# Squares of the sub-norm read from PSUM behind the value product, and the embedding's tiles placed two by two among other projections

## The chip, the cores and the metric

The kernel runs on one core of a Trainium2 chip. The metric is the time of one execution on the device, in microseconds (us). A figure below in which a trace is read belongs to one profiled execution.

## The reference, cut to what matters

```python
def reference(x, p, ...):
    h = x                                           # 512 x 1024, fp32
    for i in range(2):
        hn = rmsnorm(h, norm_mix_g[i])
        h = h + (even_mixer if i == 0 else odd_mixer)(hn, ...)
        hn = rmsnorm(h, norm_mlp_g[i])
        h = h + jnp.square(relu(hn @ w_mlp_up[i])) @ w_mlp_down[i]
        gate = sigmoid(rmsnorm(h, norm_ple_g[i]) @ w_ple_gate[i])
        h = h + (p[i] @ w_ple_proj[i]) * gate       # p[i]: 512 x 256, the embedding
    return rmsnorm(h, final_norm_g)
# even_mixer: 8 stick-breaking heads, and 4 differential heads with
#   attn = softmax1 - lam * softmax2;  o = attn @ v (128 wide)
#   o = rmsnorm(o, subln_g) * (1 - lambda_init)     # the sub-norm
# and a projection w_out of all heads' outputs
```

Layer 0 has the even mixer, layer 1 the odd one (dilated windows). The product `p[i] @ w_ple_proj[i]` depends on nothing else and may be computed at any time.

## The kernel before, in words

All matrix products keep fp32 precision by a split: an operand is rounded to a high part (`hi`, `wh`, `ph`) and what is left is a low part (`lo`, `wl`, `pl`), and `mm3` issues three matmuls, lines L138 (high times high), L141 (low of the one operand) and L142 (low of the other).

**Weights.** `wload` fetches a block of weights into a tile `raw` (two buffers); `wsplit` makes its high part on ScalarE (ACT, L122), and its low part on GpSimd (POOL, L126) in two halves, the first for k=0 and the second for k=1 of a block with two steps of contraction. The tiles `wh` and `wl` have three buffers each, and all blocks take them in turn, the two parts `ph`, `pl` of the embedding `p` among them:

```python
hi = (pool or wpool).tile([P, nk, n], F32R, tag="wh", name=nm("wh"), bufs=bufs)   # bufs = 3
lo = (pool or wpool).tile([P, nk, n], F32R, tag="wl", name=nm("wl"), bufs=bufs)
nc.scalar.activation(hi, src, AF.Copy)
for x in range(2):
    kx = slice(x * nk // 2, (x + 1) * nk // 2)
    nc.gpsimd.tensor_tensor(lo[:, kx], src[:, kx], hi[:, kx].bitcast(F32), op=ALU.subtract)
```

**Stages of the mixer.** Layer 0 has four groups of heads, in the order 2, 3, 0, 1: groups 2 and 3 are differential, 0 and 1 stick-breaking. `attend(g)` gives the attention of a group as a list of small steps, and `interleave(units, total, steps)` issues them evenly among the units of another generator, each of which is some matmuls: the projection `project` of the next group (value columns, then two blocks each of q and k). The program of a stage is then one fixed order for TensorE (PE); ACT, VectorE (DVE) and POOL follow orders that a scheduler set ahead of the run. In the last stage of layer 0, attention of group 1, the units are those of `out_first`, the first part of the output projection, four blocks of 128x768 in two halves with two output tiles each.

**The embedding's projection.** `ple_units(layer)` computes `p @ w_ple_proj` as two blocks c of four tiles of 128x512; a tile is six matmuls (k=0, 1), an evacuation from PSUM on ACT (L365) and a store to DRAM (`pjd`). All of layer 0's stand ahead of `project(1)` in the stage of attend(0); all of layer 1's stand ahead of `out_first` in the stage of attend(1). They yield once behind each three matmuls.

**The sub-norm.** Of a differential group, `combine(x)` (x = 0, 1) issues the value product into a PSUM bank `pv` and copies it to `o` (L605). Two steps later `subnorm(x)` squares `o` (L618), rounds the squares to a high part (L619), leaves the low part to DVE (L620), and sums over the partitions by two matmuls with a matrix of ones (L622, L623).

Of the kernel before, what the change touches and what calls it, by code (L numbers as in the profile page):

```python
# [3 lines left out]

# [1 line left out]

# [6 lines left out]
F32 = mybir.dt.float32  # L13
# [49 lines left out]
def trunk(  # L63
# [284 lines left out]
    def ple_units(layer):  # L348
        raw = wpool.tile([P, 2 * KT * P], F32, tag="raw", name=nm("raw"), bufs=2)
        nc.sync.dma_start(raw[:, 0:2 * S].rearrange("p (k c) -> p k c", k=2), pT[layer].rearrange("k p c -> p k c"))  # L350
        ph, pl = wsplit(raw, 0, 2, S)
        raw = wload(w_proj[layer])
        for c in range(2):
            wh, wl = wsplit(raw, c, 2, 512)
            for i in range(4):
                acc = ps("mm")
                sl = slice(i * P, (i + 1) * P)
                for k in range(2):
                    if layer < DEPTH - 1:
                        mm3(acc, wh[:, k, sl], wl[:, k, sl], ph[:, k], pl[:, k], k == 0, k == 1)  # L360
                    else:
                        mm3(acc, ph[:, k, sl], pl[:, k, sl], wh[:, k], wl[:, k], k == 0, k == 1)
                    yield 2.0
                t = mix[0].tile([P, S], F32, tag="bias", name=nm("pjt"), bufs=4) if i % 2 else t2k("tmp2")
                nc.scalar.activation(t, acc, AF.Copy)  # L365
                nc.sync.dma_start(pjd[layer, 4 * c + i], t)

    KLB = 2
    kl_i = [0]
# [2 lines left out]
    def mixer(layer, norm, nxt):  # L372
# [32 lines left out]
        lead_in = ["sc", "sc", "mm", "mm", "pv", "tp"]  # L405
        oT = [mpool.tile([P, S], F32, tag=f"o{k}", name=nm("o"), bufs=1) for k in range(KT)]

        def project(g, cur):
            kind = "dil" if layer else ("sb" if g < 2 else "diff")
            start = not first  # L410
            first.append(g)
            v = mpool.tile([P, QT, 512], F32R, tag="v", name=nm("v"), bufs=2)

            def values():
                raw = wload(next_block())
                banks = [ps(lead_in.pop(0)) if start else ps("mm") for _ in range(QT // 2)]
                accs = [b[:, c:c + 256] for b in banks for c in (0, 256)]
                for half in range(2):
                    wh, wl = wsplit(raw, half, 4, 256)
                    if half and "rcol" not in stat:  # L420
                        stat["rcol"] = tok_cols(stat["rstd"])
                    for t in range(QT):
                        for k in range(4):
                            ah, al = ahl[4 * half + k]
                            tk = slice(t * P, (t + 1) * P)
                            mm3(accs[t], ah[:, tk], al[:, tk], wh[:, k], wl[:, k],
                                half == 0 and k == 0 and t % 2 == 0, half == 1 and k == 3 and t % 2 == 1)
                            yield 1.0
                        if half == 1 and t % 2 == 1:
                            evacuate_values(t - 1, accs[t - 1])  # L430
                            evacuate_values(t, accs[t])

            def evacuate_values(t, acc):
                sc = stat["rcol"][:, t:t + 1]
                if kind == "diff":
                    src = acc
                    vh, vl = v[:, t, 0:256], v[:, t, 256:512]
                else:
                    src = acc.rearrange("p (a c) -> p a c", a=4)
                    vv = v[:, t, :].rearrange("p (a b c) -> p a b c", a=4, b=2)  # L440
                    vh, vl = vv[:, :, 0, :], vv[:, :, 1, :]
                nc.scalar.activation(vh, src, AF.Copy, scale=sc)
                nc.vector.scalar_tensor_tensor(vl, src, sc, vh.bitcast(F32), op0=ALU.mult, op1=ALU.subtract)  # L443

            heads = []

            def queries_keys():
                qscale = -0.5 * HD ** -0.5 if kind == "sb" else 0.5 * HD ** -0.5
                qk, waiting = [], []
                for isq in (True, False):  # L450
                    src = next_block()
                    lo_eng[0] = nc.vector if start else nc.gpsimd
                    blk = blk0 if isq and start and not layer else block(src, KT, P)
                    lo_eng[0] = nc.gpsimd
                    accs = [ps(lead_in.pop(0)) if start else ps("mm") for _ in range(2)]
                    if start and isq:
                        yield from lin_units(accs, blk, ahl, 0, KT, True)
                        waiting = accs
                        continue
                    if start and not layer:  # L460
                        prepare()
                    for i, acc in enumerate(accs):
                        yield from lin_units([acc], [blk[i]], ahl, 0, KT, False)
                        if waiting:
                            statistics()
                            for x, held in enumerate(waiting):
                                evacuate(True, x, held, qk, qscale)
                            waiting = []
                        evacuate(isq, i, acc, qk, qscale)

            def evacuate(isq, i, acc, qk, qscale):
                rstd = stat["rstd"]
                f = t2k("tmp")
                nc.vector.scalar_tensor_tensor(f, acc, qscale if isq else -0.5, rstd, op0=ALU.mult, op1=ALU.mult)
                lower, upper = slice(0, 64), slice(64, 128)
                if isq:
                    qq = []
                    for a, b in ((lower, upper), (upper, lower)):
                        q = mpool.tile([P, S], F32R, tag="qq", name=nm("qq"), bufs=5)
                        nc.scalar.activation(q[a], f[a], AF.Copy)  # L480
                        nc.vector.tensor_tensor(q[b], f[a], q[a].bitcast(F32), op=ALU.subtract)
                        qq.append(q)
                    qk.append(qq)
                else:
                    for s, (a, b) in enumerate(((lower, upper), (upper, lower))):
                        kl = klz[s][kl_i[0] % KLB]
                        kh = mpool.tile([P, S], F32R, tag="kh", name=nm("kh"), bufs=5)
                        nc.scalar.activation(kh[a], f[a], AF.Copy)
                        nc.scalar.activation(kh[b], f[a], AF.Copy)
                        nc.vector.tensor_tensor(kl[a], f[a], kh[a].bitcast(F32), op=ALU.subtract)  # L490
                        heads.append((qk[i][s], kh, kl))
                    kl_i[0] += 1
            cur.extend((g, kind, v, heads))
            if start:
                yield from queries_keys()
                yield from values()
            else:
                yield from values()
                yield from queries_keys()
# [55 lines left out]
        def attend(g, kind, v, heads):  # L555
# [1 line left out]
            nh = 2 if kind == "diff" else 4  # L557
            pts = [(pt_i[0] + x) % 2 for x in range(nh)]
            pt_i[0] += nh
            bias, ready = {}, {}  # L560

            def weights(x, i, evict):
                n = P * (i + 1)
# [34 lines left out]
            def combine(x):  # L598
                hi, lo = pth[pts[x]], ptl[pts[x]]
                if kind == "diff":  # L600
                    vh = lambda j: v[:, j, P * x:P * x + P]
                    vl = lambda j: v[:, j, 256 + P * x:256 + P * x + P]
                    op = pv([(vh, hi), (vh, lo), (vl, hi)])
                    o = oT[2 * g + x]
                    nc.scalar.activation(o, op, AF.Copy)  # L605
                    return
                vs = lambda j: v[:, j, P * x:P * x + P]
                op = pv([(vs, hi), (vs, lo)])
# [5 lines left out]

            def subnorm(x):
                o = oT[2 * g + x]
                hi, rs, lo = t2k("tmp2", dtype=F32R), t2k("tmp2"), t2k("tmp2", dtype=F32R)
                nc.scalar.activation(rs, o, AF.Square)  # L618
                nc.scalar.activation(hi, rs, AF.Copy)  # L619
                nc.vector.tensor_tensor(lo, rs, hi.bitcast(F32), op=ALU.subtract)  # L620
                mp = ps("pv")
                nc.tensor.matmul(mp, ones_r, hi, start=True, stop=False)  # L622
                nc.tensor.matmul(mp, ones_r, lo, start=False, stop=True)  # L623
# [29 lines left out]
                    ohl.append(split_tile(oT[tiles[len(ohl)]]))  # L653
                yield cost

        def out_first():
            for c in range(4):
                blk = block(w_outa[layer, c], 6, P)
                accs = [ps("mm") for _ in range(2)]
                for k, i in [(k, i) for k in range(6) for i in range(2)] if c == 0 else \  # L660
# [4 lines left out]
                    yield 2.0  # L665
                    if k == 5:
                        nc.vector.tensor_tensor(h[2 * c + i], h[2 * c + i], accs[i], op=ALU.add)

        cur = []
        run(project(groups[0], cur))  # L670
        for n, g in enumerate(groups[1:]):
            steps = attend(*cur)
            cur = []
            if layer == 0 and n == 2:
                interleave(chain(ple_units(0), project(g, cur)), 132.0, steps)
            else:
                interleave(project(g, cur), 100.0, steps)
        if layer == 0:
            interleave(chain(spread(ple_units(1), 2), out_first()), 100.0, attend(*cur))
        else:  # L680
            interleave(out_first(), 72.0, attend(*cur))
        ohl += [split_tile(oT[k]) for k in tiles[6:8]]
# [347 lines left out]
```

## Time and profile before

| what | value |
|---|---|
| time of the kernel, median of 3 runs | 1309.97 us (1309.74 to 1310.89) |
| time of the profiled execution | 1308.87 us |
| its span in the trace | 1307.1 us |
| granted clock, mean | 0.998 |
| stages that the change touches, in the trace | about 70 to 262 us |

The span runs from the first to the last instruction of the trace; the profiled execution took 1.8 us more, which lies around it. Busy time is the union of an engine's instructions. Matmuls are pipelined: a row's duration (0.39 us for 512 columns) is longer than the distance from one start to the next (0.23 us) where nothing is waited for, so time that PE loses is read from the distances of starts.

### The profile page before, as it was taken

The page shows a single profiled execution, that of the slowest core. Times are in us where ns is not written, and L with a number is a line of the kernel's source. Part 1 is how long each engine was busy: PE and PEld are TensorE (multiplying, and loading weights), DVE is VectorE, ACT ScalarE, POOL GpSimd, SP SyncE. Part 2 cuts the span into 40 slices and gives each one's busy share as a digit, 9 for nine tenths or more (in the row PEclk, how much of TensorE's full clock was granted, in tenths as well). Part 3 has the DMA queues.
Part 4 walks back from the last instruction along what each step waited for, and adds up shares of the span by engine and source line. Part 5 has one row for each costly group of instructions (what it writes and reads, how often), then busy time and mean ns, then how long its engine had stood idle before and what let it go on. Part 6 is the DMA issues. An engine that isn't in the chain of part 4 may idle for free.

```text
span 1307.1 us, 18561 instructions
## 1 busy us (share of the span) xinstructions
PE 1283.7 (98%) x7256; PEld 1117.4 (85%) x7256; DVE 973.5 (74%) x1623; ACT 686.0 (52%) x1117; POOL 189.8 (15%) x160
## 2 busy tenths in 40 slices
PE   9999999999999999999999999999999999999997
PEld 7988787888998989988889888788899898998876
DVE  7788888778848869845767877887784885994566
ACT  6666768554535334333456666765553443533344
POOL 2433434410000000000024333222000000000001
PEclk9999999999999999999999999999999999999999
DMA  6421423223232322323432222212223123232241
GB/s 217 135 81 50 140 93 115 89 82 112 86 108 97 102 92 97 129 97 101 157 112 96 84 89 78 69 57 95 99 97 124 70 97 129 73 122 97 97 145 65
DMA packets 28040, 133.20 MB, mean 102 GB/s; under 512 B 3312, under 2 KB 4048, under 8 KB 15280
## 3 DMA queue, kind: packets, MB, share of 16 engines
q1 hardware_dynamic: 27952, 132.01, 29.5%
q8 instruction: 57, 0.93, 0.3%
q14 instruction: 31, 0.25, 0.1%
HBM read 125.63 MB, written 6.37 MB: 101 GB/s over the span
## 4 chain that ended last, share of the span: by engine, by line
PE 85%; DVE 8%; ACT 4%; issue 1%; DMA 1%; SPq 0%; POOL 0%; ACTq 0%; DVEq 0%; POOLq 0%
PE mm L138 10%; PE mm L141 10%; PE mm L142 10%; PE sc L141 6%; PE sc L142 6%; PE sc L138 6%; PE pv L142 5%; PE pv L141 5%; PE pv L138 5%; PE tp L141 5%; PE tp L142 5%; PE tp L138 5%; PE pv L551 2%; PE tp L532 2%; PE sc L506 1%
## 5 line engine op out<-in xcount | busy, mean ns | idle before, releaser
L122 ACT ACTIVATE wh<-raw 128x1024 fp32r<-128x1024 f32 (+1 forms) x168 | 173.4, 1036 | 226.9 <-PE mm L141 63.0
L126 POOL TENSOR_TENSOR wl<-raw,wh 128x512 fp32r<-128x512 f32 (+1 forms) x132 | 177.1, 1364 | 309.3 <-ACT wh L122 303.6
L138 PE MATMUL mm<-hi,wh 128*128 128x512 f32 x472 | 187.0, 396 | 0.6 <-DVE v L443 0.4
L142 PE MATMUL mm<-hi,wl 128*128 128x512 f32 x472 | 184.8, 392 | 0.1
L141 PE MATMUL mm<-lo,wh 128*128 128x512 f32 x472 | 184.6, 391 | 0.0
L128 DVE TENSOR_TENSOR wl<-raw,wh 128x1024 fp32r<-128x1024 f32 x102 | 124.5, 1224 | 41.3 <-ACT wh L122 34.8
L142 PEld LDWEIGHTS mm<-hi,wl 128*128 128x128 f32 x472 | 88.6, 188 | 20.1 <-POOL wl L126 0.5
L138 PEld LDWEIGHTS mm<-hi,wh 128*128 128x128 f32 x472 | 88.7, 188 | 17.3 <-DVE v L443 0.6
L141 PEld LDWEIGHTS mm<-lo,wh 128*128 128x128 f32 x472 | 88.7, 188 | 15.6
L526 ACT ACTIVATE e<-e,mn 128x128 f32<-128x128 f32 (+3 forms) x96 | 53.8, 561 | 65.4 <-DVE mn L523 65.0
L754 ACT ACTIVATE wh<-raw 128x1024 fp32r<-128x1024 f32 x48 | 50.7, 1057 | 69.6 <-PE tp L141 35.1
L733 DVE TENSOR_TENSOR ul<-u,uh 128x1792 fp32r<-128x1792 f32 (+1 forms) x32 | 58.4, 1824 | 23.4 <-ACT uh L732 23.4
L732 ACT ACTIVATE uh<-u 128x1792 fp32r<-128x1792 f32 (+1 forms) x32 | 49.4, 1544 | 48.9 <-DVE u L728 48.7
L138 PE MATMUL sc<-hi,wh 128*128 128x512 f32 x184 | 71.9, 391 | 0.9 <-ACT hi L182 0.9
L141 PE MATMUL sc<-lo,wh 128*128 128x512 f32 x184 | 72.1, 392 | 0.3 <-DVE lo L183 0.3
L142 PE MATMUL sc<-hi,wl 128*128 128x512 f32 x184 | 71.8, 390 | 0.0
L721 ACT ACTIVATE u<-u 128x512 f32<-128x512 f32 x64 | 39.4, 625 | 53.8 <-DVE u L720 53.8
L142 PE MATMUL pv<-uh,wl 128*128 128x256 f32 (+1 forms) x224 | 67.4, 301 | 0.0
L142 PE MATMUL sc<-uh,wl 128*128 128x256 f32 (+1 forms) x224 | 67.3, 301 | 0.0
L141 PE MATMUL pv<-ul,wh 128*128 128x256 f32 (+1 forms) x224 | 67.2, 300 | 0.0
L141 PE MATMUL sc<-ul,wh 128*128 128x256 f32 (+1 forms) x224 | 67.2, 300 | 0.0
L138 PE MATMUL pv<-uh,wh 128*128 128x256 f32 (+1 forms) x224 | 66.6, 297 | 0.0
(259 smaller groups left out, 3645.4 us busy)
## 6 DMA issues: line engine op xcount, KB each, us to landing
raw<-in_w_up_dram SPq DMA_DIRECT2D x32, 1024.0 KB, 4.9
raw<-in_w_down_dram SPq DMA_DIRECT2D x32, 1024.0 KB, 4.9
raw<-in_w_in_dram SPq DMA_DIRECT2D x23, 1024.0 KB, 4.9
raw<-in_w_gate_dram SPq DMA_DIRECT2D x8, 1024.0 KB, 5.0
bias<-urow SPq DMA_DIRECT2D x24, 256.0 KB, 3.9
raw<-in_w_outa_dram SPq DMA_DIRECT2D x8, 768.0 KB, 4.2
pj<-pjd SPq DMA_DIRECT2D x16, 256.0 KB, 5.0
h<-in_xT_dram SPq DMA_DIRECT2D x8, 256.0 KB, 5.6
```

What stands on the lines that cost most here:

```text
L122: nc.scalar.activation(hi, src, AF.Copy)
L126: nc.gpsimd.tensor_tensor(lo[:, kx], src[:, kx], hi[:, kx].bitcast(F32), op=ALU.subtract)
L128: nc.vector.tensor_tensor(lo, src, hi.bitcast(F32), op=ALU.subtract)
L138: mm = nc.tensor.matmul(acc, lh, rh, start=start, stop=False)
L141: nc.tensor.matmul(acc, lh, rl, start=False, stop=False)
L142: nc.tensor.matmul(acc, ll, rh, start=False, stop=stop)
L526: nc.scalar.activation(e[:, 0:n], e[:, 0:n], AF.Exp, scale=-1.0, bias=mn, accum_out=s)
L532: nc.tensor.transpose(tp[:, j * P:(j + 1) * P], e[:, j * P:(j + 1) * P], ident)
L721: nc.scalar.activation(ui, ui, AF.Square, scale=0.5)
L732: nc.scalar.activation(uh[:, parts], u[:, parts], AF.Copy)
L733: nc.vector.tensor_tensor(ul[:, parts], u[:, parts], uh[:, parts].bitcast(F32), op=ALU.subtract)
L754: nc.scalar.activation(hi, src, AF.Copy)
```

## The change

The squares: `combine` now squares the PSUM bank twice, into `rs` (fp32) and into the rounded `hi`, copies `o` behind them, and forms `lo` on DVE; `subnorm` only takes these tiles up.

The embedding's tiles: of layer 0 two tiles are issued behind each of the four evacuations of q and k in `project(1)`; of layer 1 four tiles stand ahead of `out_first`, and one behind each of the first four additions to `h` in it. A tile's second yield stands behind its evacuation, and all tiles evacuate into the tag "bias" with four buffers, where every second one went to "tmp2".

```diff
@@ ple_units
-                    yield 2.0
-                t = mix[0].tile([P, S], F32, tag="bias", name=nm("pjt"), bufs=4) if i % 2 else t2k("tmp2")
+                    if k == 0:
+                        yield 2.0
+                t = mix[0].tile([P, S], F32, tag="bias", name=nm("pjt"), bufs=4)
                 nc.scalar.activation(t, acc, AF.Copy)
                 nc.sync.dma_start(pjd[layer, 4 * c + i], t)
+                yield 2.0
@@ project
-        def project(g, cur):
+        def project(g, cur, extra=iter(())):
...
                         evacuate(isq, i, acc, qk, qscale)
+                        yield from islice(extra, 4)
@@ combine (differential)
                     o = oT[2 * g + x]
+                    hi, rs, lo = t2k("tmp2", dtype=F32R), t2k("tmp2"), t2k("tmp2", dtype=F32R)
+                    nc.scalar.activation(rs, op, AF.Square)
+                    nc.scalar.activation(hi, op, AF.Square)
                     nc.scalar.activation(o, op, AF.Copy)
+                    nc.vector.tensor_tensor(lo, rs, hi.bitcast(F32), op=ALU.subtract)
+                    squares[x] = (rs, hi, lo)
                     return
@@ subnorm
-                hi, rs, lo = t2k("tmp2", dtype=F32R), t2k("tmp2"), t2k("tmp2", dtype=F32R)
-                nc.scalar.activation(rs, o, AF.Square)
-                nc.scalar.activation(hi, rs, AF.Copy)
-                nc.vector.tensor_tensor(lo, rs, hi.bitcast(F32), op=ALU.subtract)
+                rs, hi, lo = squares.pop(x)
@@ out_first
-        def out_first():
+        def out_first(extra=iter(())):
...
                         nc.vector.tensor_tensor(h[2 * c + i], h[2 * c + i], accs[i], op=ALU.add)
+                        yield from islice(extra, 2)
@@ mixer
-                interleave(chain(ple_units(0), project(g, cur)), 132.0, steps)
+                interleave(project(g, cur, ple_units(0)), 132.0, steps)
...
-            interleave(chain(spread(ple_units(1), 2), out_first()), 100.0, attend(*cur))
+            extra = ple_units(1)
+            interleave(chain(spread(islice(extra, 8), 2), out_first(extra)), 100.0, attend(*cur))
```

Three places show how this moves the instructions. A name's last number counts the tiles; `x2` stands for two such instructions in a row; lines are those of the kernel that a row is of.

The first is ACT's order around the second sub-norm (x=1) of group 3; `kh` is evacuated keys, `pv_1571` the bank with the value product. Before:

```order
L489 ACTIVATE kh_1560<-tmp_1558 64x512
L488 ACTIVATE kh_1564<-tmp_1558 64x512
L489 ACTIVATE kh_1564<-tmp_1558 64x512
L605 ACTIVATE o_206<-pv_1571 128x512
L618 ACTIVATE tmp_328_1604<-o_206 128x512
L619 ACTIVATE tmp_327_1603<-tmp_328_1604 128x512
L210 ACTIVATE tmp_328_1604<-pv_1609,eps_s 128x512
```

and of the change:

```order
L492 ACTIVATE kh_1560<-tmp_1558 64x512
L491 ACTIVATE kh_1564<-tmp_1558 64x512
L492 ACTIVATE kh_1564<-tmp_1558 64x512
L609 ACTIVATE tmp_328_1585<-pv_1571 128x512
L610 ACTIVATE tmp_327_1584<-pv_1571 128x512
L611 ACTIVATE o_206<-pv_1571 128x512
L210 ACTIVATE tmp_328_1585<-pv_1609,eps_s 128x512
```

The two squares have come to the place of the copy, the copy stands behind them, and no instruction has come between them; the rows around them are the same.

The second is PE's order where the embedding's first tiles of layer 0 stand. In the kernel before that is the start of the stage of attend(0), right behind the last matmuls of group 0's projection (`mm_1510`); `wh_1634`, `wl_1635` are the parts of `p`, `wh_1641`, `wl_1642` those of the projection's weights, c=0:

```order
L138 MATMUL mm_1510<-hi_174,wh_1504 128x512
L141 MATMUL mm_1510<-lo_175,wh_1504 128x512
L142 MATMUL mm_1510<-hi_174,wl_1505 128x512
L138 MATMUL mm_1646<-wh_1634,wh_1641 128x512
L141 MATMUL mm_1646<-wl_1635,wh_1641 128x512
L142 MATMUL mm_1646<-wh_1634,wl_1642 128x512
```

In the change they stand in the middle of that stage, behind the first q block of `project(1)` (`mm_1822`); the parts of `p` are `wh_1891`, `wl_1892`, and those of the weights `wh_1898`, `wl_1899`, which take the buffers of the q block's `wh_1812`, `wl_1813`:

```order
L138 MATMUL mm_1822<-hi_174,wh_1812 128x512
L141 MATMUL mm_1822<-lo_175,wh_1812 128x512
L142 MATMUL mm_1822<-hi_174,wl_1813 128x512
L535 MATMUL tp_1907<-ident,e_1800 128x128
L509 MATMUL sc_1911<-kh_1564,qq_1414 128x512
L510 MATMUL sc_1911<-klz_185,qq_1414 128x512
L512 MATMUL sc_1911<-sbmask,ident_r 128x128
L535 MATMUL tp_1937<-ident,e_1843 128x128 x2
L138 MATMUL mm_1903<-wh_1891,wh_1898 128x512
L141 MATMUL mm_1903<-wl_1892,wh_1898 128x512
L142 MATMUL mm_1903<-wh_1891,wl_1899 128x512
```

Between the last use of the old buffers and the first use of the new ones PE now has three transposes and one row of scores.

The third is ACT's order in the change from the end of the stage of attend(0) into that of attend(1). `wh_2304` and `wh_2311` are the embedding and its weights of layer 1, `wh_2394` and `wh_2399` the two halves of the output projection's first block, and the tiles `pjt_2278`, `pjt_2288` the last two of layer 0:

```order
L122 ACTIVATE wh_2304<-raw_2302 128x1024
L491 ACTIVATE kh_2263<-tmp_2261 64x512
L492 ACTIVATE kh_2263<-tmp_2261 64x512
L491 ACTIVATE kh_2267<-tmp_2261 64x512
L492 ACTIVATE kh_2267<-tmp_2261 64x512
L366 ACTIVATE pjt_2278<-mm_2271 128x512
L366 ACTIVATE pjt_2288<-mm_2281 128x512
L122 ACTIVATE wh_2311<-raw_2309 128x1024
L620 ACTIVATE o_200<-pv_2291 64x512
```

The split of the weights `wh_2311` stands behind seven others on ACT; its first use on PE is the first tile of layer 1.

## Rows read from the trace of the kernel before

**Rows 1.** The page's first part: the span, and of two engines the busy time, its share of the span and the instructions.

```profile
span 1307.1 us, 18561 instructions
PE 1283.7 (98%) x7256; PEld 1117.4 (85%) x7256; DVE 973.5 (74%) x1623; ACT 686.0 (52%) x1117; POOL 189.8 (15%) x160
```

**Rows 2.** Busy time by stretches. The columns are the stretch in us, its length, and busy time with the instructions of PE, the weight loads, DVE, ACT and POOL, then the granted clock, the share of the DMA engines and GB/s.

```profile
80.00:100.00 20.00, 17.16 (x100) 14.53 (x99) 15.66 (x23) 12.57 (x22) 7.43 (x5) 1.00 0.15 53
...
160.00:200.00 40.00, 40.00 (x246) 35.44 (x245) 36.05 (x51) 25.74 (x53) 15.17 (x12) 1.00 0.28 93
...
280.00:480.00 200.00, 200.00 (x1200) 179.33 (x1199) 147.90 (x185) 88.82 (x101) 0.00 (x0) 1.00 0.30 103
```

**Rows 3.** What PE waited for from 80 to 262 us: who waits on whom, then the sum in us, how often, and the longest.

```profile
PE mm L138 <- ACT tmp L365: 2.5, 2, 1.4
PE pv L622 <- ACT tmp L619: 2.4, 2, 1.2
PE sc L506 <- DVE mn L523: 1.4, 2, 1.0
PE pv L623 <- DVE tmp L620: 0.5, 2, 0.2
```

**Rows 4.** The timeline around the second sub-norm of group 3 (x=1), PE first, then ACT and DVE. The columns are the start in us from the span's start, the duration, the engine and line, the operation, and in brackets a wait and what ended it.

```profile
138.15 0.39 PE L142 MATMUL mm<-hi,wl 128*128 128x512 f32 x1
139.74 0.49 PE L622 MATMUL pv<-tmp,ones_r 128*128 128x512 f32 x1 [1.21 <-ACT tmp L619]
140.47 0.50 PE L623 MATMUL pv<-tmp,ones_r 128*128 128x512 f32 x1 [0.23 <-DVE tmp L620]
140.81 0.40 PE L138 MATMUL mm<-hi,wh 128*128 128x512 f32 x1
141.04 0.39 PE L141 MATMUL mm<-lo,wh 128*128 128x512 f32 x1
...
137.79 0.58 ACT L605 ACTIVATE o<-pv 128x512 f32<-128x512 f32 x1
138.40 0.63 ACT L618 ACTIVATE tmp<-o 128x512 f32<-128x512 f32 x1
139.06 0.63 ACT L619 ACTIVATE tmp<-tmp 128x512 fp32r<-128x512 f32 x1
139.72 0.69 DVE L620 TENSOR_TENSOR tmp<-tmp,tmp 128x512 fp32r<-128x512 f32 x1 [1.77 <-ACT tmp L619]
```

**Rows 5.** The timeline where the embedding's tiles of layer 0 begin (three rows of ACT, two of PE), and where those of layer 1 begin (the last two rows, PE).

```profile
144.84 0.22 PE L509 MATMUL sc<-sbmask,ident_r 128*128 128x128 f32 x1
146.16 0.50 PE L138 MATMUL mm<-wh,wh 128*128 128x512 f32 x1 [1.10 <-ACT tmp L365]
...
145.00 0.63 ACT L489 ACTIVATE kh<-tmp 64x512 fp32r<-64x512 f32 x1
145.54 0.57 ACT L365 ACTIVATE tmp<-mm 128x512 f32<-128x512 f32 x1
146.01 0.58 ACT L365 ACTIVATE pjt<-mm 128x512 f32<-128x512 f32 x1
...
207.23 0.33 PE L506 MATMUL sc<-kh,qq 128*128 128x256 f32 x1
209.01 0.50 PE L138 MATMUL mm<-wh,wh 128*128 128x512 f32 x1 [1.44 <-ACT tmp L365]
```

**Rows 6.** The timeline where the output projection's first block begins behind the tiles of layer 1, on PE, and the first half of that block's low part on POOL.

```profile
221.10 0.42 PE L506 MATMUL sc<-kh,qq 128*128 128x384 f32 x1
221.73 0.50 PE L138 MATMUL mm<-hi,wh 128*128 128x512 f32 x1 [0.21 <-ACT pjt L365]
222.07 0.40 PE L141 MATMUL mm<-lo,wh 128*128 128x512 f32 x1
222.56 0.50 PE L142 MATMUL mm<-hi,wl 128*128 128x512 f32 x1
222.90 0.34 PE L507 MATMUL sc<-klz,qq 128*128 128x384 f32 x1
...
221.33 1.18 POOL L126 TENSOR_TENSOR wl<-raw,wh 128x384 fp32r<-128x384 f32 x1 [4.94 <-ACT wh L122]
```

**Rows 7.** Costs: groups of instructions by line (count, busy us, mean ns of one, idle time before them and what ended it) of ACT's split and, over the whole run, of POOL's, with POOL's shortest, mean and longest in ns; and the one row that tells who waited for POOL's split.

```profile
L122 ACT ACTIVATE wh<-raw 128x1024 fp32r<-128x1024 f32 x18 | 19.0, 1056 | 2.7 <-PE mm L141 1.8 <-PE mm L142 0.5 <-issue 0.3
L126 POOL TENSOR_TENSOR wl<-raw,wh 128x512 fp32r<-128x512 f32 x100 | 140.9, 1430 | 235.1 <-ACT wh L122 229.4 <-PE pv L622 5.7
L126 POOL TENSOR_TENSOR wl<-raw,wh x132: 1007/1296/1994, 24.5 to 893.7; 128x512 fp32r<-128x512 f32 x100, 128x384 fp32r<-128x384 f32 x32
  PEld mm L142: 0.5, 1
```

**Rows 8.** The timeline of PE at three pieces of attention between projections: a transpose with a row of scores of 512 columns, a row of scores of 256 columns, and a value product.

```profile
177.06 0.27 PE L532 MATMUL tp<-ident,e 128*128 128x128 f32 x1
177.69 0.45 PE L138 MATMUL mm<-hi,wh 128*128 128x512 f32 x1
...
206.93 0.28 PE L506 MATMUL sc<-kh,qq 128*128 128x256 f32 x1
...
167.81 0.45 PE L551 MATMUL pv<-pth,v 128*128 128x512 f32 x1
169.15 0.28 PE L138 MATMUL mm<-wh,hi 128*128 128x256 f32 x1
```

More of the change, by code (lines that the diff above doesn't have):

```diff
@@ L2 @@
 from contextlib import ExitStack
-from itertools import chain
+from itertools import chain, islice
 import numpy as np
@@ L559, in attend @@
             pt_i[0] += nh
-            bias, ready = {}, {}
+            bias, ready, squares = {}, {}, {}
             def weights(x, i, evict):
```

## The prediction, as it was made before the changed kernel ran

> **What bounds the kernel now.** I read the page's first part first: PE is busy for 1283.7 of 1307.1 us, so all other engines together cost it 23.4 us, and only what changes PE's idle time can change the time [rows 1]. The table by stretches comes next, since a mean over the span hides where those 23.4 us lie. From 280 to 480 us PE works without a gap, and from 160 to 200 us too, which is attention and projection mixed as in the stretches that the change touches; from 80 to 100 us it loses 2.8 of 20 us [rows 2]. The granted clock is 1.00 in each of these. So PE is the bound where the embedding's tiles leave and also where they go. Third is the list of what PE waited for between 80 and 262 us: 2.5 us for the copy of the first embedding tile out of PSUM (L365), 2.4 and 0.5 us for the sub-norm's squares, 1.4 us for a row maximum that the change leaves alone [rows 3]. I price all losses from starts of successive matmuls: without a wait 0.23 us apart (140.81 to 141.04), and 0.34 us for the first behind a wait (140.47 to 140.81), 0.11 us more [rows 4].
>
> **Removed: the sub-norm's chain.** Between the last matmul at 138.15 and L622 at 139.74 lie 1.59 us, 1.36 too many; to L623 0.73 us, 0.50 too many; then 0.11. It happens once per differential group, at x=1. ACT works in a chain: the copy at 137.79, the square at 138.40, the rounding at 139.06 to 139.69, and L622 starts 0.05 us later; DVE's low part runs from 139.72 to 140.41 [rows 4]. In the change the two squares depend on the bank alone. Two evacuations back to back start 0.47 us apart and last 0.58 us (145.54 and 146.01) [rows 5]; no row here squares out of PSUM, and these are the nearest. So `rs` starts at 137.79, `hi` at 138.26 and ends at 138.84, L622 starts near 138.9 instead of 139.74, and L623 likewise 0.85 us sooner. I take 0.85 us for each of two groups, **−1.7**. From below: if a square out of PSUM waits for the one ahead of it (0.58 + 0.58 us instead of 0.47 + 0.58), the gain is 0.74 each, −1.5 in all; if reading the bank a second time is slow enough to eat it, 0. The copy of `o` comes 0.95 us later, and the bank is held that much longer. The next value product takes the other bank and `o` is first wanted behind L623, so I cost that at nothing; without that cover it would be at most 0.95 us each.
>
> **Removed: two waits where the tiles begin.** All layer 0 tiles stand at one place before, and the third tile's bank is free only when ACT has come through four key copies to the first tile's L365: 144.84 to 146.16 is 1.32 us, less 0.07 for the row's own 128 columns, plus 0.11 behind; I count 1.3. Where layer 1's begin, 207.23 to 209.01 is 1.78 us, less 0.12 for its 256 columns, plus 0.11: 1.8 [rows 5]. Neither place has tiles behind key copies in that form after the change. **−3.1**. A third loss, 0.9 us, stays: PE waits at 221.73 for a tile's copy and at 222.56 for POOL's half of the output weights, which ends at 222.51 [rows 6]. In the change that half block (`wh_2399`) still stands behind the tiles' copies on ACT.
>
> **Added: late splits of weights.** Three buffers serve all blocks, and the parts of `p` now keep one of them from the first tile to the last, through a whole stage of projection where before they were gone after a few us. So a block's split can begin only when the last matmul of the block ahead has let its buffer go, and PE wants the new one a few instructions later. Take the first place, the order's second piece, with s the start of the last matmul of the q block. The matmul ahead of it ends at s+0.16, ACT splits from s+0.20 for 1.06 us, and POOL makes halves of 1.43 us each [rows 7]: with 0.05 us for each handover the first is ready at s+2.74, the second at s+4.17. PE has as cover its own 0.23 us, a transpose with a row of scores (177.06 to 177.69, 0.63) and two more transposes (0.14) [rows 8], and reaches the tile at s+1.0. The tile's sixth matmul wants the second half and would start at s+2.15; it starts near s+4.2. Lost: 2.05 + 0.11, **+2.2**. The second weight block of layer 0 behind the first k block has the very same rows around it, **+2.2**.
>
> At the boundary to attend(1) the third piece of the order counts. ACT splits `p` of layer 1 from s+0.2 to s+1.26, then makes four key copies at 0.54 us (145.00 to 145.54) and two tile copies, which end near s+4.5 [rows 5]; then come the weights' split to s+5.6 and POOL's halves to s+7.05 and s+8.5 [rows 7]. PE's cover is 12 matmuls (2.74 us), a value product (167.81 to 169.15, 1.34) and two rows of 256-column scores (206.93 to 207.23, 0.30 each) [rows 5, 8]: it arrives at s+4.9, would start the tile's fifth matmul, which wants the second half here, at s+5.8 and starts it at s+8.5, **+2.8**. The second block of layer 1's projection follows the output projection's first block: its cover is a transpose with a row of scores and two matmuls more, 1.32 us, and the matmul that wants the second half would start near s+2.5 instead of s+4.2, **+1.8**. That is **+9.0** for the four places.
>
> The bounds of one place: with POOL's shortest rows, about 1.0 us for the narrower blocks, the two halves take 2.0 instead of 2.86 us, and 0.9 us less is lost; with its longest, 1.99 [rows 7], 1.1 more. I take the mean of the 128x512 row, because the hundred of them give 1430 ns. Elsewhere PE found POOL's work late for 0.5 us in the whole of that list [rows 7], which says that buffers were free early, not that POOL is quick. The other moves (tags, loads that change places in SP's queue, yields) I cost at nothing: stores and loads run under projection matmuls; a late load would cost PE its lateness.
>
> The sum: −1.7 −3.1 +9.0 = **+4.2**. The profiled execution took 1308.87 us, 1.8 more than its span, so 1313.1 for its like; it lay 1.1 us under the median of 1309.97, so I forecast **1314.2**.
>
> The Trainium skill, "Perfetto Trace Analysis", section on identifying performance opportunities, says that interleaving regimes in which different engines are the most contended may help. By it, spreading the tiles should pay, and the sum would be the −4.8 of the two removals. The same section reads a bubble that keeps coming back on the engine that should be saturated as a sign of too few buffers for the next tile; by that the change costs time. The trace agrees with the second so far as it goes: PE is the contended engine on both sides.
>
> **Rivals.** *The covers hold, and it is faster.* The place is the first use of `wh_1898` and its three likes: if their splits start when data is there rather than at the last matmul of the block ahead, nothing new waits, and −4.8 is left, or −2.0 with the boundary's 2.8 alone: 1305.2 to 1308.0, say 1306. It decides in this sense where the four losses together stay under 2.2 us. For it: 160 to 200 us without a gap, with splits in it [rows 2], and a POOL that idled 235 us waiting for ACT [rows 7]. Against it: three buffers, of which one is taken. Chance 0.14. The Trainium skill's rule on interleaving regimes, above, would stand with this rival.
>
> *No change.* Short halves and one or two of the four covered: the losses come to between 2.2 and 7.4 us and balance the gains, 1309.97 ± 2.6, with 1311 in the middle. For it: every fault in the cover, a row more of scores at one place, is worth 0.6 us. Chance 0.22.
>
> *The squares gain nothing* because a bank read three times is no quicker than SBUF, or because ACT's queue holds them: +5.9, 1315.9. Against it are evacuations of 0.58 us against 0.63 for SBUF to SBUF [rows 4]. Chance 0.08.
>
> *POOL's late halves run long,* at 1.99 us each since DVE works beside them: 1.1 us more at each of four places, +8.6, 1318.6. Chance 0.06. My forecast itself, 1312.7 to 1317, gets 0.50.
>
> **From cases to numbers.** Of this kernel 0.2% is 2.6 us, about what a measurement can tell from no change; below 1307.35 is faster, above 1312.6 slower. Faster 0.14, same 0.22, slower 0.64. The range leaves out the long halves above (0.06) and most of the faster case below (about 0.12): 1307.0 to 1317.5; the likeliest case's own is 1312.7 to 1317.
>
> **What would show it.** L622 at x=1 starting 0.75 us behind the last matmul instead of 1.59, with squares 0.47 us apart on ACT; no wait of 1 us ahead of the first tile behind the key copies; four waits of PE's weight load on POOL's L126, of 1 to 2.8 us, each with an L122 just ahead whose releaser is a matmul. The prediction is wrong if PE waits for L126 no more than before, if L122 of these blocks starts well ahead of the block's last matmul, or if a row of the attention that I took for unaffected begins to wait for ACT behind a split.

## The result, and the profile after

The changed kernel takes 1316.03 us, median of five runs (1315.36 to 1316.78), against 1309.74 us of the kernel before, taken beside it (five runs, 1309.38 to 1310.89): a ratio of 1.0047, 95% interval 1.0032 to 1.0062. It is 6.3 us slower. The forecast was 1314.2 us, slower, in a range of 1307.0 to 1317.5.

The page's first part for the changed kernel, beside [rows 1]:

```profile
span 1314.3 us, 18577 instructions
PE 1287.0 (98%) x7256; PEld 1116.7 (85%) x7256; DVE 976.4 (74%) x1623; ACT 685.3 (52%) x1117; POOL 191.0 (15%) x160
```

PE was idle for 27.3 us of the span where before it was for 23.4. The other 3.3 of the 7.2 us count as busy: the row ahead of a wait is not overlapped after 0.23 us by the next but runs its 0.39 us to the end, and the row behind a wait lasts 0.50 us instead of 0.39. For twelve new waits that makes some 3.2 us. What PE waited for from 60 to 270 us of the changed kernel, to be held against [rows 3]:

```profile
PE mm L142 <- POOL wl L126: 2.8, 5, 0.6
PE mm L141 <- POOL wl L126: 2.2, 4, 0.7
PE mm L138 <- ACT wh L122: 1.6, 3, 0.8
PE sc L509 <- DVE mn L526: 1.4, 2, 1.1
PE pv L627 <- ACT tmp L610: 0.7, 2, 0.4
PE mm L138 <- ACT pjt L366: 0.5, 1, 0.5
PE mm L138 <- DVE v L445: 0.5, 1, 0.5
...
```

The two waits for the first tiles' copies (2.5 us) are gone, the sub-norm's 2.4 us are down to 0.7, and the first three rows are new: 6.6 us in twelve waits, all for a part of a weight block. The row maximum's 1.4 us is as it was.

**The sub-norm after** (x=1 of group 3, PE, then ACT), the answer to [rows 4]:

```profile
138.14 0.39 PE L142 MATMUL mm<-hi,wl 128*128 128x512 f32 x1
138.89 0.50 PE L627 MATMUL pv<-tmp,ones_r 128*128 128x512 f32 x1 [0.36 <-ACT tmp L610]
139.61 0.50 PE L628 MATMUL pv<-tmp,ones_r 128*128 128x512 f32 x1 [0.22 <-DVE tmp L612]
139.95 0.40 PE L138 MATMUL mm<-hi,wh 128*128 128x512 f32 x1
...
137.78 0.58 ACT L609 ACTIVATE tmp<-pv 128x512 f32<-128x512 f32 x1
138.26 0.58 ACT L610 ACTIVATE tmp<-pv 128x512 fp32r<-128x512 f32 x1
138.73 0.58 ACT L611 ACTIVATE o<-pv 128x512 f32<-128x512 f32 x1
```

From the last projection matmul to L627 it is 0.75 us instead of 1.59, and the two squares start 0.48 us apart: 0.84 us less, twice, as the prediction's sum had it.

**The first late split** (two tiles of layer 0 behind the first q block; PE, ACT, POOL):

```profile
162.04 0.39 PE L142 MATMUL mm<-hi,wl 128*128 128x512 f32 x1
...
162.91 0.38 PE L535 MATMUL tp<-ident,e 128*128 128x128 f32 x2
163.56 0.50 PE L138 MATMUL mm<-wh,wh 128*128 128x512 f32 x1 [0.27 <-ACT wh L122]
163.90 0.39 PE L141 MATMUL mm<-wl,wh 128*128 128x512 f32 x1
164.91 0.50 PE L142 MATMUL mm<-wh,wl 128*128 128x512 f32 x1 [0.62 <-POOL wl L126]
...
165.49 0.40 PE L141 MATMUL mm<-wl,wh 128*128 128x512 f32 x1
166.46 0.50 PE L142 MATMUL mm<-wh,wl 128*128 128x512 f32 x1 [0.57 <-POOL wl L126]
...
162.07 0.49 ACT L594 ACTIVATE e<-sc 128x384 f32<-128x384 f32 x1 [0.46 <-DVE e L598]
162.45 1.05 ACT L122 ACTIVATE wh<-raw 128x1024 fp32r<-128x1024 f32 x1
...
163.58 2.83 POOL L126 TENSOR_TENSOR wl<-raw,wh 128x512 fp32r<-128x512 f32 x2 [3.67 <-ACT wh L122]
```

The chain is to be read upward from 166.46: it waits for POOL's second half, POOL began when ACT ended at 163.50, and ACT could not begin before the q block let the buffer go: the last matmul that reads its high part, the one ahead of 162.04, ends near 162.20. ACT began at 162.45, behind a row of attention that had itself waited for DVE until 162.07. So the last thing ahead of the split in this trace is ACT's order and not the matmul; that the buffer puts the split at this place in the order is shown by the run with more buffers, below. PE loses 0.51 us ahead of 163.56 (two transposes take 0.14), 0.78 ahead of 164.91, 0.74 ahead of 166.46, and 0.11 behind each: 2.4 us.

**The boundary to attend(1)** (PE, then ACT):

```profile
207.91 0.22 PE L512 MATMUL sc<-sbmask,ident_r 128*128 128x128 f32 x1
208.94 0.73 PE L138 MATMUL mm<-wh,wh 128*128 128x512 f32 x2 [0.81 <-ACT wh L122]
210.30 0.50 PE L141 MATMUL mm<-wl,wh 128*128 128x512 f32 x1 [0.63 <-POOL wl L126]
...
210.86 0.40 PE L138 MATMUL mm<-wh,wh 128*128 128x512 f32 x1
211.54 0.50 PE L141 MATMUL mm<-wl,wh 128*128 128x512 f32 x1 [0.28 <-POOL wl L126]
...
213.05 0.40 PE L142 MATMUL mm<-wh,wl 128*128 128x512 f32 x1
213.93 0.50 PE L138 MATMUL mm<-wh,wh 128*128 128x512 f32 x1 [0.48 <-ACT pjt L366]
...
207.83 1.06 ACT L122 ACTIVATE wh<-raw 128x1024 fp32r<-128x1024 f32 x1
...
212.55 0.85 ACT L122 ACTIVATE wh<-raw 128x768 fp32r<-128x768 f32 x1 [2.02 <-DMA raw<-in_w_outa_dram]
213.30 0.58 ACT L366 ACTIVATE pjt<-mm 128x512 f32<-128x512 f32 x1
```

In place of the one wait of before for a bank [rows 5] stand three for the weights' parts: 0.97, 0.79 and 0.45 us, and 0.11 behind each, 2.5 us. Behind them comes one that the prediction did not have: ACT waits 2.02 us for the load of the output weights, the tile's copy is queued behind that split, and PE wants the copy's bank at 213.93, 0.65 + 0.11 us late.

### The profile page after: what moved, and what is told of

Its sections match the earlier page's. It is cut to its first block, busy times and chain, and to the rows that moved or that the text cites. A ratio compares the mean times of both kernels' runs of the same rounds, so it can differ in the third digit from the quotient of the medians.

```text
span 1314.3 us, 18577 instructions
## 1 busy us (share of the span) xinstructions
PE 1287.0 (98%) x7256; PEld 1116.7 (85%) x7256; DVE 976.4 (74%) x1623; ACT 685.3 (52%) x1117; POOL 191.0 (15%) x160
## 4 chain that ended last, share of the span: by engine, by line
PE 78%; DVE 4%; ACT 1%; issue 1%; POOL 1%; ACTq 0%; POOLq 0%; DVEq 0%
PE mm L142 9%; PE mm L141 9%; PE mm L138 9%; PE sc L142 5%; PE sc L141 5%; PE sc L138 5%; PE pv L142 5%; PE pv L141 5%; PE pv L138 5%; PE tp L141 5%; PE tp L142 5%; PE tp L138 5%; PE pv L554 2%; PE tp L535 1%; PE sc L510 1%
## 5 line engine op out<-in xcount | busy, mean ns | idle before, releaser
L122 ACT ACTIVATE wh<-raw 128x1024 fp32r<-128x1024 f32 (+1 forms) x168 | 173.4, 1037 | 228.9 <-PE mm L141 60.0
L740 DVE TENSOR_TENSOR ul<-u,uh 128x1792 fp32r<-128x1792 f32 (+1 forms) x32 | 58.4, 1824 | 23.4 <-ACT uh L739 23.4
```

The lines of the kernel that those rows point to most:

```text
L740: nc.vector.tensor_tensor(ul[:, parts], u[:, parts], uh[:, parts].bitcast(F32), op=ALU.subtract)
```

## The experiments

Losses below are worked out from starts of matmuls, as in the prediction; times are medians against the kernel before on the same chip, 1309.32 us for the first four and 1309.71 us for the rest. The changed kernel's 1316.03 us belongs to 1309.74, so where one of the first four is set against it, the difference carries 0.4 us of doubt.

**The squares alone.** The edit is that of `combine` and `subnorm`, and nothing else.

> The kernel before with the squares of the sub-norm read from PSUM, and nothing else. If the gain on PE is kept to the end: two times 0.85 us, 1308.0 us against 1309.7 of before. If what PE gains there is waited for again later in the stage: 1309.7 us, unchanged.

Measured: 1308.27 us, ratio 0.9990 (0.9981 to 0.9999), a gain of 1.05 us. At the stage it is 1.6 us: the matmul behind the 145 us bank wait starts at 144.56 instead of 146.16, and the first tile behind the boundary at 207.42 instead of 209.01. The spans differ by 1.1 us. So some 0.5 us was lost again later, far behind the change: about 0.2 us near 282 us, and 0.3 us at 793.58, where a value product waits 0.22 us for DVE (L541) and in the kernel before only 0.07.

**The tiles' places alone.** The changed kernel, with the sub-norm put back:

```diff
-                    nc.scalar.activation(rs, op, AF.Square)
-                    nc.scalar.activation(hi, op, AF.Square)
...
+                nc.scalar.activation(rs, o, AF.Square)
+                nc.scalar.activation(hi, rs, AF.Copy)
```

> The changed kernel with the sub-norm as it was before, so that only the embedding's tiles are moved. Theory (the two parts add, and the tiles' new places cost all of the loss and more): 1316.0 + 1.7 = 1317.7 us. Rival (the squares' copy to o, which comes later, delays a bank and is part of the loss): under 1316.0 us.

Measured: 1318.17 us, ratio 1.0064 (1.0051 to 1.0076). The places cost 8.9 us, and the squares take 2.1 us of it off (2.6 if each kernel is set against its own kernel before). Measured one by one the two parts come to +7.8 us, together to +6.3; with intervals of about 1.2 us or more to either side, that does not speak against a plain sum. The rival, a delay by the later copy to `o`, wanted a time under 1316.0 us and is not seen.

**Buffers for the embedding's parts.**

```diff
-        ph, pl = wsplit(raw, 0, 2, S)
+        ph, pl = ([mix[0].tile([P, S], F32R, tag="bias", name=nm("ple"), bufs=4) for _ in range(2)] for _ in range(2))
+        for k in range(2):
+            src = raw[:, k * S:(k + 1) * S]
+            nc.scalar.activation(ph[k], src, AF.Copy)
+            nc.gpsimd.tensor_tensor(pl[k], src, ph[k].bitcast(F32), op=ALU.subtract)
...
-                t = mix[0].tile([P, S], F32, tag="bias", name=nm("pjt"), bufs=4)
+                t = t2k("tmp2")
```

> The changed kernel, but the split parts of the embedding p lie in four tiles of the tag bias, which stand idle in these two stages, and the copies of the tiles go to tmp2; so all three buffers of wh and wl serve weight blocks. The tiles stand where the change puts them. Theory (late splits for want of a buffer): the three waits inside the stages, measured at 2.3, 2.4 and 2.1 us, are gone, and with them 6.8 us: 1309.2 us, and down to 1307 if the wait at the boundary goes too. Rival (other work of PE, ACT and DVE collides at the new places, whatever the buffers): 1315 to 1316 us.

Measured: 1314.66 us, ratio 1.0036 (1.0024 to 1.0049): 1.4 us better than the changed kernel, between the two expectations and nearer to the rival's. The trace tells why. The three waits in question are gone: PE loses 0.2 us there where it lost 2.4 and 2.7, and nothing at the second block of layer 1's tiles. With the third buffer free, the split of the first tile's weights stands 6.4 us ahead of the tile, which now follows the q block without a gap (ACT, then PE):

```profile
155.77 1.09 ACT L122 ACTIVATE wh<-raw 128x1024 fp32r<-128x1024 f32 x1
...
161.92 0.40 PE L142 MATMUL mm<-hi,wl 128*128 128x512 f32 x1
162.15 0.40 PE L138 MATMUL mm<-ple,wh 128*128 128x512 f32 x1
```

But what was gained is waited for a few us later. Behind the key block PE comes sooner to a matmul that wants the bank of a tile whose copy stands on ACT behind a split, four key copies and two rows of attention (PE, then ACT):

```profile
192.23 0.28 PE L558 MATMUL pv<-ptl,v 128*128 128x256 f32 x1
194.53 0.50 PE L138 MATMUL mm<-hi,wh 128*128 128x512 f32 x1 [2.02 <-ACT tmp L370]
...
196.03 0.63 PE L142 MATMUL mm<-hi,wl 128*128 128x512 f32 x1
196.45 0.63 PE L138 MATMUL mm<-hi,wh 128*128 128x512 f32 x1
...
189.35 1.06 ACT L122 ACTIVATE wh<-raw 128x1024 fp32r<-128x1024 f32 x1 [1.64 <-PE mm L142]
...
193.90 1.07 ACT L370 ACTIVATE tmp<-mm 128x512 f32<-128x512 f32 x2
```

That is 2.18 us. The split at 189.35 had itself waited 1.64 us for a matmul, so a want of buffers for weights is a part of this wait too; a fourth buffer was not tried. Behind the wait the matmuls start 0.42 us apart for some 3 us, of which the section on the hardware tells more. A transpose loses 0.71 us to a wait for DVE at 150.93, and at the boundary 1.5 us are still lost, now for the parts of `p`. And from 216.05 to 219.53 us the waits for POOL's halves of the output weights cost 1.2 us more than in the changed kernel (losses of 0.68 and 1.31 us instead of 0.30 and 0.52). So late splits are the cause of those three waits, which this run shows by taking them away; a placement of tiles that pays needs ACT's queue to be free as well.

**DVE in POOL's place for the tiles' weights.**

```diff
-        if lo_eng[0] is nc.gpsimd:
+        if lo_eng[0] is nc.gpsimd and not dve:
...
             nc.vector.tensor_tensor(lo, src, hi.bitcast(F32), op=ALU.subtract)
...
-            wh, wl = wsplit(raw, c, 2, 512)
+            wh, wl = wsplit(raw, c, 2, 512, dve=True)
```

> The changed kernel, but the low part of the two weight blocks of each embedding projection is made by DVE in one instruction (1.22 us in the profile) instead of by POOL in two of 1.43 us. The split starts as late as before. Theory (PE waits for ACT's split and then for POOL's two halves, one after the other): each of the four waits shrinks from 2.1 to 2.4 us to 1.0 to 1.3 us, 4 to 4.6 us in all: 1311.4 to 1312 us. If the start alone set the loss, and POOL's time did not count: 1316 us.

Measured: 1313.56 us, ratio 1.0032 (1.0019 to 1.0044), 2.5 us better than the changed kernel. At the places themselves the theory holds: behind the q block 1.2 us are lost (0.49 + 0.51, and twice 0.11) instead of 2.4, behind the k block 1.4 instead of 2.7, at the second block of layer 1 some 0.7 instead of 2.3. PE's waits:

```profile
PE mm L138 <- ACT pjt L366: 1.8, 1, 1.8
...
PE mm L142 <- DVE wl L128: 0.5, 2, 0.3
```

The first row is where most of the rest went: at the boundary PE, now sooner, waits 1.8 us instead of 0.5 for the tile's copy behind the late load, whose split starts 3.6 us behind the boundary's first tile in both kernels (209.75 and 206.12 here, 212.55 and 208.94 in the changed one). And behind that wait the granted clock fell, as the section on the hardware tells.

**One layer's tiles at a time.** In the changed kernel, first layer 1's tiles are put back, then, in another kernel, layer 0's:

```diff
-            extra = ple_units(1)
-            interleave(chain(spread(islice(extra, 8), 2), out_first(extra)), 100.0, attend(*cur))
+            interleave(chain(spread(ple_units(1), 2), out_first()), 100.0, attend(*cur))
```

```diff
-                interleave(project(g, cur, ple_units(0)), 132.0, steps)
+                interleave(chain(ple_units(0), project(g, cur)), 132.0, steps)
```

> The changed kernel, but layer 1's tiles all stand ahead of the output projection as before. Theory (each late split costs by itself): the wait at the second block of layer 1's tiles, 2.1 us in the profile of the changed kernel, goes, the two in layer 0's and the one at the boundary stay: 1316.0 - 2.1 = 1313.9 us. If the layer 1 part carried the loss, it would be near 1310 us.

Measured: 1313.21 us, ratio 1.0026 (1.0016 to 1.0036), 2.8 us under the changed kernel where 2.1 was expected; the waits of the q and k blocks and of the boundary stand as in the changed kernel's trace.

> The changed kernel, but layer 0's tiles all stand ahead of project(1) as before. Theory: the squares alone gave 1308.3 us; the wait for the second block of layer 1's tiles comes on top with 2.1 us, and the waits at 145 us (1.3) and at the boundary (1.8) stand as before: 1310.4 us. If layer 0's part did no harm, it would be near 1314 to 1316 us.

Measured: 1312.62 us, ratio 1.0026 (1.0015 to 1.0037), 2.2 us above the expectation. Of that, some 1.5 us lie in a wait that I had not thought of (ACT, then PE):

```profile
154.44 0.60 ACT L366 ACTIVATE pjt<-mm 128x512 f32<-128x512 f32 x1 [2.02 <-DMA pjd<-pjt]
...
153.46 0.40 PE L142 MATMUL mm<-wh,wl 128*128 128x512 f32 x1
155.09 0.50 PE L138 MATMUL mm<-wh,wh 128*128 128x512 f32 x1 [1.22 <-ACT pjt L366]
```

With all tiles in the tag "bias" the fifth copy needs a buffer whose store to DRAM has not landed, and PE waits for the copy: 1.40 + 0.11 us. What is left, 0.7 us, is not traced to a wait; the profiled execution, the slowest of the seven, also ran at the lower clock from 16 to 19 us, ahead of all that the change touches. So the change of tag, which the prediction costed at nothing, costs 1.5 us when the tiles stand together, as they did before; in the changed kernel itself the tiles are far enough apart in layer 0, and no such wait is in its list.

**A version that beats both.** The squares, the old places, and other PSUM banks for the first two tiles of each layer:

```diff
-                acc = ps("mm")
+                acc = ps("tp" if c == 0 and i < 2 else "mm")
```

> The kernel before with the squares read from PSUM, the embedding's tiles at their old places, and the first two tiles of each layer in the two banks of tag tp instead of mm, so that the third tile finds its bank free while ACT is still at the key copies. Theory (the waits of 1.3 and 1.8 us there are for a bank and for nothing else): 1308.3 - 3.1 = 1305.2 us. If the matmuls behind them then wait for the same ACT queue in another way: 1307 to 1308.3 us.

Measured: 1306.49 us, ratio 0.9976 (0.9966 to 0.9985): 3.2 us faster than the kernel before, 9.5 us faster than the changed one. Of the 3.1 us of bank waits some 1.3 came back as smaller waits in the same places (PE, both stages):

```profile
146.25 0.40 PE L142 MATMUL mm<-wh,wl 128*128 128x512 f32 x1
147.16 0.44 PE L506 MATMUL sc<-kh,qq 128*128 128x384 f32 x1 [0.51 <-ACT e L591]
...
208.45 0.40 PE L142 MATMUL mm<-wh,wl 128*128 128x512 f32 x1
209.25 0.50 PE L138 MATMUL mm<-wh,wh 128*128 128x512 f32 x1 [0.40 <-ACT tmp L365]
```

0.68 and 0.57 us, both for ACT, which works without a pause there: at the first place 1.28 us of its work, from 145.37, is a load of its table (`ACT_TABLE_LOAD`, L590) ahead of the awaited row. So half the rival was true too.

## Why the prediction was right, point by point

**The sub-norm** was right in mechanism and size: −1.7 us at the stage in the trace, −1.05 us in time alone and −2.1 us on top of the places, where 1.7 was forecast.

**The two bank waits** of 1.3 and 1.8 us at the old places are gone from the changed kernel's list, as forecast.

**The late splits** were right in mechanism at all four places, and the terms sized thus: behind the q block 2.2 forecast and 2.4 measured; behind the k block 2.2 and 2.7 (two transposes from 190.12 end at 190.26, the tile starts at 191.05; then 191.38 to 192.40 and 192.97 to 193.96, with 0.11 behind each); at the boundary 2.8 and 2.5; at the second block of layer 1 1.8 and 2.3 (229.59 to 230.08, 230.65 to 231.62 and 232.19 to 233.18). Together 9.0 and 9.9. The step that was short is ACT's start: the prediction let the split begin 0.20 us behind the start of the block's last matmul, and it began 0.41 us behind it at the q block, 0.79 at the k block (189.95 against 189.16) and 0.51 at layer 1's second block (228.95 against 228.44). Each time ACT had a row of attention to do first, at the q block from 162.07 to 162.56. So one sign that the prediction named, an L122 whose releaser is a matmul, is not in the trace at these three; and the forecast waits of 1 to 2.8 us came as two or three waits each, of 0.27 to 0.81 us.

**What was costed at nothing** makes most of the difference. A wait of 0.61 + 0.11 us for a value evacuation (L445) at 155.09 is new; the tile's copy behind the late load of the output weights costs 0.76; the half block of output weights costs 1.0 instead of 0.9. That is 1.6 us. With 9.9 and −4.8 the sum is +6.7 us on PE in the trace, against +4.2 forecast and a median that is 6.3 us up. The spans differ by 7.2, but 0.9 us of that arose ahead of anything that the change touches: in its profiled execution the changed kernel waits at 13.43 and 14.29 us for the high and the low part of an operand, 0.59 and 0.36 us, where the execution of before does not, and at 80 us it stands 0.9 us behind. That leaves 6.3.

**The rivals.** That the covers hold is refuted by the twelve waits of the list. No change is refuted by the ratio's interval and by losses of 9.9 us at the four places, more than its 7.4. Squares that gain nothing are refuted by the squares alone: narrowly by the time (a ratio of 0.9981 to 0.9999), plainly by the trace. Long halves did not occur at these places: POOL took 2.83 us for two at both places of layer 0 and 2.53 at the boundary, 1.42 and 1.27 each on the mean instead of 1.99. The Trainium skill, "Perfetto Trace Analysis", section on identifying performance opportunities, reads a bubble that keeps coming back on the engine that should be saturated as a possible want of buffers for the next tile. The run with buffers for the embedding's parts agrees: the bubbles of 2.4 to 2.7 us went. Its rule that interleaving regimes may help speaks of regimes in which the most-contended engine changes; here it was PE on both sides, and the tiles' new places cost 8.9 us.

## What to carry to other kernels

Moving independent work into gaps pays only if its operands' preparation also finds its place: look at whose buffer the operand takes over, which matmul lets that go, and how much work stands on the bound engine between that matmul and the first use, against the whole chain of split and halves. A tile that stays live across a stage takes a buffer from every block in it. And when a wait is taken away, read which instruction of the same slow queue the bound engine will meet next: here three repairs handed a third or more of their gain on (1.4 us came of 6.8, 2.5 of 4 to 4.6, 1.8 of 3.1), in good part to ACT's queue and some of it to the clock.

## What the runs showed of the hardware

A wait can cost more than its length. Behind the 2.18 us wait of the kernel with buffers for the embedding's parts the granted clock fell to the lower of its two levels for about 3 us (stretch in us, length, busy time of PE, weight loads, DVE, ACT and POOL, then the clock):

```profile
194.00:195.00 1.00, 0.47 (x2) 0.42 (x3) 0.97 (x2) 1.00 (x4) 0.00 (x0) 1.00 0.00 0
195.00:196.00 1.00, 1.00 (x5) 0.77 (x4) 0.96 (x2) 0.95 (x3) 0.00 (x0) 0.76 0.67 252
196.00:197.00 1.00, 1.00 (x4) 0.78 (x3) 1.00 (x3) 0.82 (x2) 0.00 (x0) 0.50 0.73 273
197.00:198.00 1.00, 1.00 (x5) 0.70 (x4) 1.00 (x3) 0.35 (x2) 0.00 (x0) 0.50 0.09 16
...
199.00:200.00 1.00, 1.00 (x6) 0.81 (x5) 0.79 (x2) 0.59 (x2) 0.00 (x0) 1.00 0.00 0
```

At 0.50 (1.2 GHz) the matmuls of 512 columns start 0.42 us apart instead of 0.23 at 1.00 (2.4 GHz), and this one costs some 1.6 us (the losses of seven successive starts from 195.60 to 198.80). PE had been idle for most of 2.2 us ahead of it. The same stretch follows the boundary's waits in the kernel with the moved tiles alone, in the one with DVE's low half and in the one with layer 0's tiles moved, whose granted clocks are 0.57, 0.64 and 0.68 on the mean from 212 to 216 us; in the profiled execution of the changed kernel the boundary's waits were of like length and the clock stayed at 1.00. So waits of like length bring it in one execution and not in another.

It also comes far from the change. In the kernel with the squares and other banks the clock fell behind two waits of PE in layer 1's attention, 1.27 and 0.52 us, that end at 841.84 and 842.86:

```profile
843.00:846.00 3.00, 3.00 (x10) 2.71 (x11) 2.30 (x4) 1.90 (x4) 2.19 (x2) 0.50 0.00 0
```

The kernel before has the same two waits (1.28 and 0.52 us, up to 844.50 and 845.51), and its clock stayed at 1.00. The profiles with buffers for the embedding's parts and with DVE's low half have this stretch too, at 851 us. What it does to a time can be read from the executions: of the ten with other banks, the four with a mean granted clock of 0.998 took 1305.71 to 1306.14 us, the six with 0.997 took 1306.32 to 1307.29. The five with buffers for the embedding's parts are all at 0.996 or 0.997, those of the changed kernel at 0.997 or 0.998. So where two medians here lie about 1 us apart, a part of that can be how often the clock fell.
